# The order of the attention units in a hybrid encoder block: two heads by turns, scores by pairs

## The chip, the cores and the metric

The kernel runs on one core of a Trainium2 chip. Its time is the device time of one execution in microseconds (us), from the first to the last instruction and what lies around them; the metric is the median of several runs. The engines are the matrix engine (PE, with its weight loads shown apart as PEld), the vector engine (DVE), the scalar engine (ACT), GpSimd (POOL) and the engine that issues the transfers (SP). Each has an instruction stream of its own, and they meet through semaphores.

## What is computed

One layer of an encoder with 1024 tokens of width 1024. One projection gives the columns of two groups of eight heads of 64, and each group's output is gated and projected back:

```python
h = x @ w_in                                   # q_a k_a v_a z_a q_b k_b v_b z_b
y_a = neighborhood_attention(q_a, k_a, v_a, rel_bias)      # 2-D window 8 x 16 on a 16 x 64 grid
y_b = windowed_gqa_with_sink(rotary(q_b), rotary(k_b), v_b, sink)   # |i - j| <= 128, 2 kv heads
mixed = concat(y_a * silu(z_a), y_b * silu(z_b))
x = layer_norm(alpha * x + mixed @ w_out)
```

In the b group a softmax row also holds a learned sink logit. In the a group a learned bias is added to each score.

## The kernel before, in words

All products are made in 16-bit pieces: a value is split into a high and a low half, and a product is the sum of high times high, high times low and low times high. A projection of 128 columns thus takes 2 x 24 matmuls of 512 columns (L405).

Three stages follow each other: values and the first six projections (to about 123 us), the attention (to about 357 us), and the output projection with the layer norm (`final`). The remaining 15 projections and the first products of the output are not a stage of their own: they are a list of work, `FILL`, from which `pump_to` takes a share at each step of the attention, by the step numbers in `FILL_AT`, so that PE always has something to do.

The attention consists of 128 units, written out in `unit_list`, and its loop has a step for each. A unit is 128 queries of one head. Heads go by pairs p = 0 to 3, with j = 0 or 1 in the pair. The b group comes first: 16 units for a pair, first the eight query blocks i of j = 0, then those of j = 1. A block looks at three key blocks (384 columns), blocks 0 and 7 at two (256). The a group has 16 units for a pair too: for each j four column strips b (windows of 24, 32, 32 and 24 grid columns) of two row halves each.

At step i the loop does this, in program order, which every engine keeps (the stage is written in a manual schedule):

- `stage_load` for unit i + 7: for an a unit of half 0 and b not 2 it issues the bias load (L878) and queues the scaling on POOL (L882). A ring of BR = 5 buffers holds the biases.
- `stage_qk(i)`: two matmuls into one of four PSUM banks "s" that are used in turn, q against the high keys (L910) and q against the low keys (L911). q holds its high half in 64 rows and its low half in the other 64, and the keys lie in both, so that one product over 128 rows gives two of the terms. Then one DVE instruction adds mask or bias and finds the row's extreme (L920); for b units of blocks 0 and 1 a copy of one column puts the sink in place first (L915).
- for the quad whose turn it is (four units in a row, nine steps after its first unit): `stage_ot` of the quad before (four transposes on PE, L995, and the product with the gate, L998 or L1004), `stage_pv` (the weighted sums, 33 or 36 matmuls of 64 columns, L975).
- `stage_tr(i - 1)`: the high half of the probabilities on ACT (L946), the low half on DVE (L947), and a transposing transfer (L950). L947 is the last reader of the score bank.
- `stage_on` one step after `stage_pv`: reciprocal and product with the row sums (L981, L984).
- `stage_exp(i)`: the exponential on ACT (L936), written back into the score bank.

Around these the loop takes operations from queues for ACT, DVE, POOL and SP: the evacuation of finished projections (L281 to L289 and L319 for q and k, L335 to L339 for the rotary, L362 to L366 for gates), the splitting of the next weights, transfers. `need` puts out at once what has not been taken when it is needed; before a unit it is called for the stacks of its head. The values of the a group are gathered from DRAM for the next pair (`gather_v`, L834) at the steps of `VA_STEP`.

Of the kernel before, what the change touches and what calls it, by code (L numbers as in the profile page):

```python
# [17 lines left out]
HD = 64  # L18
# [24 lines left out]
Z3_END = 119  # L43
WIN_AT = [186, 202, 218, 234]
VA_AT = [46, 49, 52, 55]
VA_STEP = [(0, 1, 1), (0, 1, 3), (1, 0, 1), (1, 0, 3)]
# [21 lines left out]
def hybrid_block(ctx, tc, xT, x, wt, wv, wo, bias, sink, gain, lbias, cos, sin, bmask, out):  # L68
# [238 lines left out]
    def split_k(p, half, src, dep=None):  # L307
        sl = slice(512 * half, 512 * half + 512)
        ops = []
        prio = 0 if dep is None else 1  # L310
        eng = "pool" if dep and clock["step"] is not None else "dve"
        for j in range(2):
            a, o = slice(64 * j, 64 * j + 64), slice(64 - 64 * j, 128 - 64 * j)
            hi, lo = split_hl(lambda j=j, a=a: own("kh", p, j)[a, sl], lambda j=j, a=a: own("kl", p, j)[a, sl],
                              src[a], dep is None, eng)

            def dup_(w, j=j, a=a, o=o):
                t = own(w, p, j)
# [5 lines left out]
            dup = [enq("pool", lambda d=dup_: d("kh"), o1, after=32 if dep else 0),  # L324
                   enq("pool", lambda d=dup_: d("kl"), o2, after=36 if dep else 0)]
            stk_ops.setdefault((p, j, half), []).extend(dup)
        return ops

# [529 lines left out]
    on = {}  # L858

    def geom(u):  # L860
        g, p, j, t, _ = u
        if g == "a":
            b, half = t
            w = WINW[b]
            return NKEY[b], [4 * w] * 3
        lo, hi = max(t - 1, 0), min(t + 2, 8)
        return 128 * (hi - lo), [128] * (hi - lo)

    def stage_load(u, i):
        g, p, j, t, _ = u  # L870
        n, _c = geom(u)
        if g == "a":
            b, half = t
            if half == 0 and b != 2:
                bulk["last"] = clock["step"] + 1
                bt = ap.tile([128, 23 * WINW[1]], F32, tag="bs", name="bias", bufs=BR)
                o, m = BOFF[b], 23 * WINW[b]
                nc.sync.dma_start(bt[:, :m], bias[2 * p + j, :, o:o + m])  # L878
                bv = bt[:, :m]
                ld = Op("sp", None, [], 1)  # L880
                ld.step = i
                op = enq("pool", lambda: nc.gpsimd.tensor_scalar(bv, bv, rsg, -1.0, op0=ALU.mult, op1=ALU.mult),  # L882
                         ld, prio=0)
                st["bias"] = bt, op
            o = 11 * WINW[b] * half
            st[u, "b"] = st["bias"][0][:, o:o + NROW[half] * WINW[b]], st["bias"][1]

    def stage_qk(u):
        g, p, j, t, _ = u
        n, _c = geom(u)  # L890
        ps = bank("s")
        m, end = n, 384
        if g == "a":
            b, half = t
            m, end = NROW[half] * WINW[b], 384 if half else 384 - WINW[1]
            q = stks["q", p, j][:, 512 * half + 128 * b:512 * half + 128 * b + 128]
            sl = [stks[w, p, j].rearrange("p (r c) -> p r c", c=GW)[
                :, 4 * half:4 * half + NROW[half], WIN0[b]:WIN0[b] + WINW[b]] for w in ("kh", "kl")]
            bias_t, op = st.pop((u, "b"))
            need(op)  # L900
            init = 3e38
        else:
            q = stks["q", f"b{p}", j][:, 128 * t:128 * t + 128]
            lo = max(t - 1, 0) * 128
            kv = p // 2
            sl = [stks[w, "b", kv][:, lo:lo + n] for w in ("kh", "kl")]
# [3 lines left out]
        nc.tensor.matmul(ps[:, :m], q, sl[0], start=True, stop=False)  # L910
        nc.tensor.matmul(ps[:, :m], q, sl[1], start=False, stop=True)  # L911
        s0 = sns[units.index(u) % 2]
        sn = s0[:, end - m:]
        if g == "b" and t < 2:
            nc.vector.tensor_copy(s0[:, 384:385], nsk[:, h:h + 1])  # L915
# [4 lines left out]
        nc.vector.tensor_tensor_reduce(sn[:, :m], ps[:, :m], bias_t, sg[:, c:c + 1], init,  # L920
                                       op0=ALU.add, op1=ALU.min, accum_out=nm)
        st[u, "sn"] = sn
        st[u, "ps"] = ps
        st[u, "nm"] = nm

    def stage_exp(u):
        n, _c = geom(u)
        m = n + 1 if u[0] == "b" else n
        sn, nm = st.pop((u, "sn")), st.pop((u, "nm"))
        pt = st.pop((u, "ps"))  # L930
        k = units.index(u) % 4
        if k == 0:
            st["sm"] = ap.tile([128, 4], F32, tag="sm", name="sm", bufs=4)
        sm = st["sm"]
        st[units.index(u) // 4, "sm"] = sm
        nc.scalar.activation(pt[:, :m], sn[:, :m], AF.Exp, bias=nm, scale=-1.0, accum_out=sm[:, k:k + 1])  # L936
        st[u, "p"] = pt

    def stage_tr(u):
        g, p, j, t, _ = u  # L940
        n, ch = geom(u)
        pt = st.pop((u, "p"))
        c, m = ch[0], len(ch)
# [7 lines left out]
        st[u, "tr"] = tr  # L951

    def quad(q):
        g, p, j, t, _ = units[4 * q]
        return g, p, j, t // 4 if g == "b" else t[0] // 2

    def stage_pv(q):
        ps = st[q, "o"] = bank("t")
        for m in range(4):
            u = units[4 * q + m]  # L960
            g, p, j, t, _ = u
            n, ch = geom(u)
            tr = st.pop((u, "tr"))
            c = ch[0]
# [1 line left out]
            for i in range(len(ch)):  # L966
# [4 lines left out]
                    v = [vb[:, max(t - 1, 0) + i, p // 2, e, :] for e in range(2)]  # L971
                ph, pl = tr[:c, 2 * i, :], tr[:c, 2 * i + 1, :]
                mms += [(ph, v[0]), (ph, v[1]), (pl, v[0])]
            for i, (a, b_) in enumerate(mms):
                nc.tensor.matmul(ps[:, HD * m:HD * m + HD], a, b_, start=(i == 0), stop=(i == len(mms) - 1))  # L975

    def stage_on(q):
        g, p, j, h = quad(q)
        ps = st.pop((q, "o"))
        ri = ap.tile([128, 4], F32, tag="ri", name="ri", bufs=4)  # L980
        nc.vector.reciprocal(ri, st.pop((q, "sm")))  # L981
        if j == 0:
            on[g, p, h] = ap.tile([128, 4, 2, HD], F32, tag="on", name="on", bufs=2)
        nc.vector.tensor_mul(on[g, p, h][:, :, j, :], ps[:, :4 * HD].rearrange("p (m e) -> p m e", e=HD),  # L984
                             ri.unsqueeze(2).to_broadcast([128, 4, HD]))

    def stage_ot(q):
        g, p, j, h = quad(q)
        if j == 0:
            return  # L990
        need(*stk_ops.get(f"zb{p}" if g == "b" else f"z{p}", ()))
        ps = bank("t")
        o = on.pop((g, p, h))
        for i in range(4):
            nc.tensor.transpose(ps[:, 128 * i:128 * i + 128], o[:, i].rearrange("p h e -> p (h e)"), identf)  # L995
# [275 lines left out]
    for i in range(-LD, NU + LO):  # L1271
# [31 lines left out]
        if bulk["last"] != i or (queues["sp"] and i - queues["sp"][0].born > 2):  # L1303
            pop("sp", 1 if i < 118 else 3)
        if i < NU:
            u = units[i]
            if u[3] in (0, 4):
                need(*stk_ops[f"b{u[1]}", u[2], u[3] // 4])
            if u[3] == (0, 0):
                need(*stk_ops[u[1], u[2], 0], *stk_ops[u[1], u[2], 1])  # L1310
            stage_qk(u)
        q, m = divmod(i - LP - 3, 4)
        if i >= Q30 + 2:
            q, m = (NU // 4 - 2, i - Q30 - 2) if i < Q30 + 4 else divmod(i - LP - 3, 4)
        elif i >= Q30:
            q, m = -1, 0
        if m == 0 and 0 <= q - 1 < NU // 4:
            stage_ot(q - 1)
        if m == 0 and 0 <= q < NU // 4:
            stage_pv(q)  # L1320
        if i > Z3_END:
# [9 lines left out]
            wo_scale(i - WO_MAX - 4)  # L1331
        pump_to(i + F1)
        if 0 <= q < NU // 4:
            g, p, j, h = quad(q)
# [90 lines left out]
```

## Time and profile before

| what | us |
|---|---|
| median of 3 runs | 447.07 |
| lowest and highest | 446.6, 447.26 |
| the profiled execution | 447.43 |
| its span, first to last instruction | 445.6 |
| PE busy | 438.6 |
| PEld busy | 254.3 |
| DVE busy | 345.7 |
| ACT busy | 309.0 |
| POOL busy | 227.0 |

Busy times of different engines lie beside each other. A matmul's row shows when it started; its length is modelled and longer than the distance to the next start, because matmuls are pipelined. In a view of groups stand line, engine, operation, output and inputs, shape, count, busy time, mean ns of one, and the idle time ahead of them with what ended it. In a view in order of time stand start, length and the instruction, and in brackets the idle time before it. In a view of stretches stand the stretch, its length, the busy time of PE, PEld, DVE, ACT and POOL with their counts, the granted clock of PE, the share of the DMA engines and GB/s. A row of transfers ends with KB each, where it is known, and the median us from issue to landing.

### The profile page before, as it was taken

The page shows a single profiled execution, that of the slowest core. Times are in us where ns is not written, and L with a number is a line of the kernel's source. Part 1 is how long each engine was busy: PE and PEld are TensorE (multiplying, and loading weights), DVE is VectorE, ACT ScalarE, POOL GpSimd, SP SyncE. Part 2 cuts the span into 40 slices and gives each one's busy share as a digit, 9 for nine tenths or more (in the row PEclk, how much of TensorE's full clock was granted, in tenths as well). Part 3 has the DMA queues.
Part 4 walks back from the last instruction along what each step waited for, and adds up shares of the span by engine and source line. Part 5 has one row for each costly group of instructions (what it writes and reads, how often), then busy time and mean ns, then how long its engine had stood idle before and what let it go on. Part 6 is the DMA issues. An engine that isn't in the chain of part 4 may idle for free.

```text
span 445.6 us, 9522 instructions
## 1 busy us (share of the span) xinstructions
PE 438.6 (98%) x3271; PEld 254.3 (57%) x3271; DVE 345.7 (78%) x862; ACT 309.0 (69%) x718; POOL 227.0 (51%) x240
## 2 busy tenths in 40 slices
PE   9999999999999999999999999999999999999994
PEld 8996754444445555565655655655555654444442
DVE  5969967829989787786898888897767747279954
ACT  6769459877488998798979978797886876002211
POOL 0002753565837758868507628667762446005740
PEclk9999999999999999999999999999999999999999
DMA  8972068976847887678989999999999888101721
GB/s 306 348 286 94 1 242 270 298 268 238 285 138 165 149 179 163 141 146 133 165 164 173 194 182 184 201 188 239 189 189 229 156 190 323 49 0 71 253 79 71
DMA packets 133984, 81.76 MB, mean 183 GB/s; under 512 B 101296, under 2 KB 113328, under 8 KB 133680
## 3 DMA queue, kind: packets, MB, share of 16 engines
q1 hardware_dynamic: 133504, 80.67, 74.1%
q8 instruction: 25, 0.41, 0.4%
q10 hardware_dynamic: 432, 0.49, 0.3%
q14 instruction: 23, 0.19, 0.2%
HBM read 50.73 MB, written 9.96 MB: 136 GB/s over the span
## 4 chain that ended last, share of the span: by engine, by line
PE 88%; DMA 6%; ACT 3%; DVE 1%; issue 0%; SPq 0%; ACTq 0%; DVEq 0%
PE ps_pj L405 47%; PE ps_s L1122 9%; PE ps_t L975 7%; PE ps_pj L1122 5%; PE ps_t L1122 5%; PE ps_s L910 4%; PE ps_s L911 4%; PE ps_s L662 3%; PE ps_t L995 2%; PE ps_t L662 1%; DMA wos<-in_wo 1%; PE ps_pj L662 1%; DMA wr<-in_wt 1%; DMA x<-in_xT 1%; ACT wf L511 1%; DMA wvraw<-in_wv 1%
## 5 line engine op out<-in xcount | busy, mean ns | idle before, releaser
L405 PE MATMUL ps_pj<-xf,wh 128*128 128x512 f16 x672 | 202.6, 379 | 0.1
L405 PE MATMUL ps_pj<-xf,wl 128*128 128x512 f16 x336 | 127.3, 379 | 0.0
L405 PEld LDWEIGHTS <-wh 128*128 128x128 f16 x672 | 63.9, 98 | 60.3 <-issue 0.5
L936 ACT ACTIVATE ps_s<-sn,nm 128x385 f32<-128x385 f32 (+3 forms) x128 | 70.0, 547 | 28.9 <-DVE nm L920 27.8
L947 DVE SCALAR_TENSOR_TENSOR split<-ps_s,split 128x384 f16<-128x384 f32 (+2 forms) x128 | 65.6, 512 | 16.9 <-ACT split L946 16.0
L1122 PEld LDWEIGHTS <-m 128*128 128x128 f16 x408 | 38.8, 98 | 42.7 <-issue 0.2
L946 ACT ACTIVATE split<-ps_s 128x384 f16<-128x384 f32 (+2 forms) x128 | 57.6, 450 | 2.4
L405 PEld LDWEIGHTS <-wl 128*128 128x128 f16 x336 | 32.9, 98 | 36.7
L920 DVE CUSTOM_DVE_ANT_0 sn<-ps_s,bias,sg 128x264 f32<-128x264 f32 (+1 forms) x64 | 35.2, 549 | 15.8 <-PE ps_s L911 5.3
L212 POOL TENSOR_SCALAR wr<-wr,wsc 128x512 f32<-128x512 f32 x26 | 22.1, 851 | 41.1 <-ACT wh L207 35.5
L920 DVE CUSTOM_DVE_ANT_0 sn<-ps_s,bm,nsk 128x384 f32<-128x384 f32 (+1 forms) x64 | 40.7, 636 | 1.8 <-PE ps_s L911 1.3
L1122 PE MATMUL ps_s<-wo,m 128*128 128x512 f16 (+1 forms) x192 | 42.0, 372 | 0.0
L910 PE MATMUL ps_s<-ks,qs 128*128 128x384 f16 (+4 forms) x128 | 39.2, 306 | 0.0
L882 POOL TENSOR_SCALAR bias<-bias,rsg 128x552 f32<-128x552 f32 (+1 forms) x24 | 18.7, 779 | 40.3 <-DMA bias<-in_bias 32.0
L911 PE MATMUL ps_s<-ks,qs 128*128 128x384 f16 (+4 forms) x128 | 39.2, 306 | 0.0
L975 PEld LDWEIGHTS <-tr 128*128 128x128 f16 (+1 forms) x1104 | 36.6, 98 | 2.2
L1179 ACT ACTIVATE sd<-mv,eps 128x1 f32<-128x1 f32 x8 | 2.4, 295 | 44.3 <-DVE mv L1177 42.0
L213 POOL TENSOR_TENSOR wl<-wr,wh 128x512 f16<-128x512 f32 x26 | 31.6, 1215 | 2.2
L1221 POOL TENSOR_TENSOR xr<-xr,gb 128x512 f32<-128x512 f32 x7 | 11.2, 1608 | 39.7 <-ACT xr L1218 39.7
L319 POOL COPY ks<-ks 64x512 f16<-64x512 f16 x40 | 26.0, 662 | 4.7 <-DVE ks L289 1.8
L558 POOL TENSOR_SCALAR xraw<-xraw,xsc 128x512 f32<-128x512 f32 x3 | 4.9, 1645 | 41.0 <-ACT xf L553 41.0
L1122 PE MATMUL ps_pj<-wo,m 128*128 128x512 f16 (+1 forms) x120 | 25.2, 347 | 0.0
(208 smaller groups left out, 840.3 us busy)
## 6 DMA issues: line engine op xcount, KB each, us to landing
ws<-in_wt SPq DMA_DIRECT2D x15, 512.0 KB, 5.7
wr<-in_wt SPq DMA_DIRECT2D x26, 256.0 KB, 3.7
bias<-in_bias SPq DMA_DIRECT2D x16, 276.0 KB, 3.4
wor<-in_wo SPq DMA_DIRECT2D x16, 256.0 KB, 3.6
xr<-in_x SPq DMA_DIRECT2D x8, 512.0 KB, 8.1
xraw<-in_xT SPq DMA_DIRECT2D x15, 256.0 KB, 5.0
out<-xr SPq DMA_DIRECT2D x14, 256.0 KB, 2.1
bias<-in_bias SPq DMA_DIRECT2D x8, 368.0 KB, 3.8
```

What stands on the lines that cost most here:

```text
L213: nc.gpsimd.tensor_sub(l, raw, h)
L319: nc.gpsimd.tensor_copy(t[o, sl], t[a, sl])
L405: nc.tensor.matmul(ps, a[:, k % 4, :], mv, start=(k == 0 and i == 0), stop=(k == KT - 1 and i == 2))
L662: nc.tensor.matmul(ps[:, :320], lh[1, k][:, 128 * t:128 * t + 128], rh[k][:, 320 * a:320 * a + 320], start=(k == 0 and i == 0), stop=(k == ...
L910: nc.tensor.matmul(ps[:, :m], q, sl[0], start=True, stop=False)
L911: nc.tensor.matmul(ps[:, :m], q, sl[1], start=False, stop=True)
L920: nc.vector.tensor_tensor_reduce(sn[:, :m], ps[:, :m], bias_t, sg[:, c:c + 1], init, op0=ALU.add, op1=ALU.min, accum_out=nm)
L936: nc.scalar.activation(pt[:, :m], sn[:, :m], AF.Exp, bias=nm, scale=-1.0, accum_out=sm[:, k:k + 1])
L946: nc.scalar.activation(hl[:, :m, 0, :c], src, AF.Copy, scale=PSCALE)
L947: nc.vector.scalar_tensor_tensor(hl[:, :m, 1, :c], src, PSCALE, hl[:, :m, 0, :c], op0=ALU.mult, op1=ALU.subtract)
L975: nc.tensor.matmul(ps[:, HD * m:HD * m + HD], a, b_, start=(i == 0), stop=(i == len(mms) - 1))
L1122: nc.tensor.matmul(ps, lh[:, ts], rh[:, cs], start=(e == EO[0] and i == 0), stop=(e == EO[-1] and i == 2))
```

## The change

The units of a pair alternate between its heads: in the b group block i of j = 0, then block i of j = 1; in the a group, for each strip, (half, j) = (0, 0), (1, 1), (0, 1), (1, 0). The score products of two units are put out together at every even step, high keys for both and then low keys for both; the rest of `stage_qk` stays at the unit's own step. The stacks of both heads are asked for ahead of the pair's first unit. The sink's column is copied for block 0 alone, since each head now keeps its own of the two score tiles. A quad now holds both heads, so its output goes into one half of a tile of eight, and `stage_ot` follows for two quads at once, at every odd quad. Biases are kept for each j, loaded when the strip changes, in a ring of six. Values are gathered one strip a quad.

```diff
-LTT, LPP, BP, BH, BR, ND, NA, NX, F1 = 1, 6, 2, 9, 5, 1, 1, 6, 0.2
+LTT, LPP, BP, BH, BR, ND, NA, NX, F1 = 1, 6, 2, 9, 6, 1, 1, 6, 0.2
...
         for p in range(4):
-            for j in range(2):
-                for i in range(8):
-                    us.append(("b", p, j, i, i % 2 == 1))
+            for i in range(8):
+                for j in range(2):
+                    us.append(("b", p, j, i))
         for p in range(4):
-            for j in range(2):
-                for b in range(4):
-                    for half in range(2):
-                        us.append(("a", p, j, (b, half), half == 1))
+            for b in range(4):
+                for half, j in ((0, 0), (1, 1), (0, 1), (1, 0)):
+                    us.append(("a", p, j, (b, half)))
...
-            if half == 0 and b != 2:
+            key = p, j, b - (b == 2)
+            if st.get(("bias", j), (None,))[0] != key:
...
+    def stage_mm(us):
+        for u in us:
+            m, q, sl = qk_parts(u)
+            ps = st[u, "ps"] = bank("s")
+            nc.tensor.matmul(ps[:, :m], q, sl[0], start=True, stop=False)
+        for u in us:
+            m, q, sl = qk_parts(u)
+            nc.tensor.matmul(st[u, "ps"][:, :m], q, sl[1], start=False, stop=True)
...
-        nc.tensor.matmul(ps[:, :m], q, sl[0], start=True, stop=False)
-        nc.tensor.matmul(ps[:, :m], q, sl[1], start=False, stop=True)
...
-        if g == "b" and t < 2:
+        if g == "b" and t == 0:
             nc.vector.tensor_copy(s0[:, 384:385], nsk[:, h:h + 1])
...
-        if j == 0:
-            on[g, p, h] = ap.tile([128, 4, 2, HD], F32, tag="on", name="on", bufs=2)
-        nc.vector.tensor_mul(on[g, p, h][:, :, j, :], ps[:, :4 * HD].rearrange("p (m e) -> p m e", e=HD),
+        if q % 2 == 0:
+            on[q // 2] = ap.tile([128, 2, 4, HD], F32, tag="on", name="on", bufs=2)
+        nc.vector.tensor_mul(on[q // 2][:, q % 2], ps[:, :4 * HD].rearrange("p (m e) -> p m e", e=HD),
...
         if i < NU:
-            u = units[i]
-            if u[3] in (0, 4):
-                need(*stk_ops[f"b{u[1]}", u[2], u[3] // 4])
-            if u[3] == (0, 0):
-                need(*stk_ops[u[1], u[2], 0], *stk_ops[u[1], u[2], 1])
-            stage_qk(u)
+            if i % 2 == 0:
+                us = units[i:i + 2]
+                for u in us:
+                    if u[3] in (0, 4):
+                        need(*stk_ops[f"b{u[1]}", u[2], u[3] // 4])
+                    if u[0] == "a" and i % 16 == 0:
+                        need(*stk_ops[u[1], u[2], 0], *stk_ops[u[1], u[2], 1])
+                stage_mm(us)
+            stage_qk(units[i])
...
-        if m == 0 and 0 <= q - 1 < NU // 4:
-            stage_ot(q - 1)
+        if m == 0 and (3 <= q < NU // 4 and q % 2 == 1 or q == NU // 4):
+            stage_ot(q - 3 if q < NU // 4 else q - 2)
...
-            if g == "a" and p < 3 and (j, h, m) in VA_STEP:
-                gather_v(p + 1, VA_STEP.index((j, h, m)))
+            if g == "a" and p < 3 and m == 1:
+                gather_v(p + 1, b)
```

More of the change, by code (lines that the diff above doesn't have):

```diff
@@ L860, in geom @@
     def geom(u):
-        g, p, j, t, _ = u
+        g, p, j, t = u
         if g == "a":
@@ L883, in stage_load, with qk_parts @@
                          ld, prio=0)
-                st["bias"] = bt, op
+                st["bias", j] = key, bt, op
             o = 11 * WINW[b] * half
-            st[u, "b"] = st["bias"][0][:, o:o + NROW[half] * WINW[b]], st["bias"][1]
+            _, bt, op = st["bias", j]
+            st[u, "b"] = bt[:, o:o + NROW[half] * WINW[b]], op
+    def qk_parts(u):
+        g, p, j, t = u
+        n, _c = geom(u)
+        if g == "a":
+            b, half = t
+            q = stks["q", p, j][:, 512 * half + 128 * b:512 * half + 128 * b + 128]
+            sl = [stks[w, p, j].rearrange("p (r c) -> p r c", c=GW)[
+                :, 4 * half:4 * half + NROW[half], WIN0[b]:WIN0[b] + WINW[b]] for w in ("kh", "kl")]
+            return NROW[half] * WINW[b], q, sl
+        q = stks["q", f"b{p}", j][:, 128 * t:128 * t + 128]
+        lo = max(t - 1, 0) * 128
+        return n, q, [stks[w, "b", p // 2][:, lo:lo + n] for w in ("kh", "kl")]
+    def stage_mm(us):
[6 more added lines that the diff above has]
+            nc.tensor.matmul(st[u, "ps"][:, :m], q, sl[1], start=False, stop=True)
     def stage_qk(u):
-        g, p, j, t, _ = u
+        g, p, j, t = u
         n, _c = geom(u)
-        ps = bank("s")
+        ps = st[u, "ps"]
         m, end = n, 384
@@ L973, in stage_pv @@
                 mms += [(ph, v[0]), (ph, v[1]), (pl, v[0])]
+            o = HD * slot(u)
             for i, (a, b_) in enumerate(mms):
-                nc.tensor.matmul(ps[:, HD * m:HD * m + HD], a, b_, start=(i == 0), stop=(i == len(mms) - 1))
+                nc.tensor.matmul(ps[:, o:o + HD], a, b_, start=(i == 0), stop=(i == len(mms) - 1))
     def stage_on(q):
-        g, p, j, h = quad(q)
         ps = st.pop((q, "o"))
```

40 lines of the change are left out of this document (16 added, 24 removed).

## The prediction

> **What bounds the kernel now.** I read the page first, then busy time by stretch, then the matrix engine's instructions in order of time.
>
> ```profile
> span 445.6 us, 9522 instructions
> PE 438.6 (98%) x3271; PEld 254.3 (57%) x3271; DVE 345.7 (78%) x862; ACT 309.0 (69%) x718; POOL 227.0 (51%) x240
> ...
> PE 88%; DMA 6%; ACT 3%; DVE 1%; issue 0%; SPq 0%; ACTq 0%; DVEq 0%
> ```
>
> The chain that ended last is 88% PE. A stretch of the attention (busy time of PE, PEld, DVE, ACT, POOL) leaves PE no idle time, and vector and scalar engine little:
>
> ```profile
> 123.00:153.00 30.00, 29.89 (x238) 16.19 (x236) 25.60 (x83) 26.29 (x65) 19.32 (x18) 1.00 0.69 150
> 183.00:213.00 30.00, 30.00 (x268) 17.09 (x264) 22.27 (x64) 25.54 (x70) 21.98 (x23) 1.00 0.79 141
> ```
>
> Ends of matmuls are modelled, so 98% alone proves nothing; the starts do. PE in order of time, around units 47 to 49 (start, length, line, shape):
>
> ```profile
> 208.86 0.27 PE L910 MATMUL ps_s<-ks,qs 128*128 128x256 f16 x1
> 208.97 0.27 PE L911 MATMUL ps_s<-ks,qs 128*128 128x256 f16 x1
> 209.08 0.59 PE L405 MATMUL ps_pj<-xf,wh 128*128 128x512 f16 x2
> 209.51 0.38 PE L405 MATMUL ps_pj<-xf,wl 128*128 128x512 f16 x1
> ...
> 210.37 0.27 PE L910 MATMUL ps_s<-ks,qs 128*128 128x256 f16 x1
> 210.48 0.27 PE L911 MATMUL ps_s<-ks,qs 128*128 128x256 f16 x1
> ...
> 211.89 0.33 PE L910 MATMUL ps_s<-ks,qs 128*128 128x384 f16 x1
> 212.05 0.33 PE L911 MATMUL ps_s<-ks,qs 128*128 128x384 f16 x1
> ```
>
> Two products of 512 columns start 0.43 us apart (209.08 to 209.51), 0.215 us each; 256 columns take 0.11 (210.37 to 210.48), 384 take 0.16 (211.89 to 212.05). That is 0.42 to 0.43 ns a column throughout: PE streams without holes. Weight loads are hidden, and the second product into a bank is no dearer than the first. So PE work sets the time, and a wait of PE in the attention lengthens it one for one.
>
> The Trainium skill, Perfetto Trace Analysis, section Identifying the Most-Contended Engine, calls matmul busy time a bad measure of headroom and takes the busy share of weight loads instead, here 57%. By it PE would have much to gain from regrouping; the trace, with its even spacing, disagrees.
>
> **The change, part by part.**
>
> *Products.* Each unit keeps its two score products with the same columns, its weighted sums and its share of the transposes. Removed and added PE work is 0 us. Only the order is new: at an even step kh(i), kh(i+1), kl(i), kl(i+1), at an odd step none. PE starts even steps when it did before.
>
> *Score banks.* This is the disputed cost. There are four "s" banks, unit u uses bank u mod 4, and the bank is free when L947 (the low half of the split) of unit u-4 has read it. Before, an odd unit u asks for its bank at its own step. Now it asks one step earlier, right behind kh(u-1). Even units ask as before. So for each odd u I compare the end of L947 of unit u-4 with the score product of u-1. Unit 49 first (DVE in order of time):
>
> ```profile
> 209.55 0.69 DVE L366 SCALAR_TENSOR_TENSOR z<-z,ps_pj 128x512 f32<-128x512 f32 x1 [1.73 <-ACT z L365]
> 210.15 0.67 DVE L920 CUSTOM_DVE_ANT_0 sn<-ps_s,bm,nsk 128x384 f32<-128x384 f32 x1
> 210.75 0.55 DVE L947 SCALAR_TENSOR_TENSOR split<-ps_s,split 128x384 f16<-128x384 f32 x1
> 211.76 0.53 DVE L920 CUSTOM_DVE_ANT_0 sn<-ps_s,bm,nsk 128x256 f32<-128x256 f32 x1
> ```
>
> The 256-column L920 is unit 47 (block 7). The L947 ahead of it belongs to unit 45 and ends at 210.75 + 0.55 = 211.30. Unit 49 asked at 211.89: 0.59 us to spare. Now it asks at 210.37 + 0.11 = 210.48: **0.82 us too early**. Unit 45 is that late for a reason the change leaves in place (ACT, then POOL):
>
> ```profile
> 208.83 0.69 ACT L365 ACTIVATE z<-ps_pj,invt 128x512 f32<-128x512 f32 x1 [1.60 <-POOL rp_raw L337]
> 207.53 1.27 POOL L337 TENSOR_TENSOR rp_raw<-rp_raw,cos 128x512 f32<-128x512 f32 x1
> ```
>
> The gate of zb3 goes into the tile of the cosines, so it waits for the last rotary product at 208.80, and the exponential of unit 45 is queued behind it. The other two places are units 9 and 17:
>
> ```profile
> 136.56 0.27 PE L910 MATMUL ps_s<-ks,qs 128*128 128x256 f16 x1
> 137.86 0.33 PE L910 MATMUL ps_s<-ks,qs 128*128 128x384 f16 x1
> 136.65 0.55 DVE L947 SCALAR_TENSOR_TENSOR split<-ps_s,split 128x384 f16<-128x384 f32 x1
> 149.94 0.27 PE L910 MATMUL ps_s<-ks,qs 128*128 128x256 f16 x1
> 149.90 0.55 DVE L947 SCALAR_TENSOR_TENSOR split<-ps_s,split 128x384 f16<-128x384 f32 x1
> ```
>
> Unit 5 frees its bank at 136.65 + 0.55 = 137.20; unit 9, due at 137.86, would ask at 136.56 + 0.16 = 136.72 (unit 8 has 384 columns in the new order): 0.48 short. Unit 13 frees at 150.45; unit 17 would ask at 149.94 + 0.11 = 150.05: 0.40 short. Over these units DVE lags PE, so both count from one baseline: not 0.88 but the larger.
>
> The order also shifts where blocks 0 and 7 (256 columns, L920 0.53 instead of 0.67 us, about 0.27 with L947) fall: units 0, 1, 14, 15 of a pair instead of 0, 7, 8, 15. Unit 1 is lighter, so 0.27 less at unit 9; by unit 13 one light unit fewer has run, 0.27 more at unit 17 (0.67). For the first two places I take the middle, 0.5. For unit 49 the lighter unit 33 may bring the chain 0.27 forward: 0.82 - 0.27 = 0.55. Whether the two add depends on DVE having caught up with PE between them; I add them, since a shift of PE then moves the evacuations behind it too.
>
> In the second group the room is larger. Unit 64 asks at 239.51, and unit 61 (the L947 here, before block 7's) ends at 238.90:
>
> ```profile
> 239.51 0.28 PE L910 MATMUL ps_s<-ks,qs 128*128 128x264 f16 x1
> 238.34 0.56 DVE L947 SCALAR_TENSOR_TENSOR split<-ps_s,split 128x384 f16<-128x384 f32 x1
> ```
>
> Unit 65 then has 0.61 + 0.11 us in hand, so from here on I count 0.
>
> *The start.* PE waits once behind unit 0, for a projection bank:
>
> ```profile
> 123.59 0.27 PE L911 MATMUL ps_s<-ks,qs 128*128 128x256 f16 x1
> 123.98 0.59 PE L405 MATMUL ps_pj<-xf,wh 128*128 128x512 f16 x2
> 123.24 0.69 DVE L366 SCALAR_TENSOR_TENSOR z<-z,ps_pj 128x512 f32<-128x512 f32 x1 [0.29 <-ACT z L365]
> ```
>
> Instead of 0.11 it takes 0.39 to the next start, 0.28 of waiting. Two more products of 0.11 now lie in this hole: -0.22. The baseline above is absolute and already holds it, so it counts only if units 9 and 17 do not wait.
>
> *Earlier needs.* Both heads' stacks are needed at the pair's first unit, eight steps sooner for the second head. The tightest are the first pair's q (DVE) and q2 (DVE, then PE at unit 96):
>
> ```profile
> 120.32 2.63 DVE L289 TENSOR_TENSOR qs<-rp_raw,qs 64x512 f16<-64x512 f32 x2
> 295.34 0.69 DVE L287 SCALAR_TENSOR_TENSOR qs<-ps_pj,qs 64x512 f16<-64x512 f32 x1
> 298.29 0.28 PE L910 MATMUL ps_s<-ks,qs 128*128 128x264 f16 x1
> ```
>
> They end at 122.95, ahead of unit 0 at 123.48 (0.11 before the row of 123.59), and at 296.03, ahead of 298.29: 0 us, with 0.5 and 2.3 us of cover.
>
> *Vector engine.* Eight one-column copies go, one a pair for each head:
>
> ```profile
> L915 DVE COPY sn<-nsk 128x1 f32<-128x1 f32 x16 | 2.3, 144 | 0.0
> ```
>
> That is 8 x 0.144 = 1.2 us of DVE over the whole attention, beside PE: 0. The gate products move up to four steps later, to every second quad.
>
> *Transfers.* The 24 bias loads and 16 value gathers keep their number and sizes. Bias loads now come at two steps running instead of spread (lead 7 steps as before, a sixth buffer):
>
> ```profile
> bias<-in_bias SPq DMA_DIRECT2D x16, 276.0 KB, 3.4
> va<-vwin SPq DMA_DIRECT2D x8, 256.0 KB, 3.4
> tr<-split SPq DMA_TRANSPOSE x128, 3.3
> ...
> L882 POOL TENSOR_SCALAR bias<-bias,rsg 128x552 f32<-128x552 f32 (+1 forms) x24 | 18.7, 779 | 40.3 <-DMA bias<-in_bias 32.0 <-DVE split L947 6.8 <-ACT ks L281 0.7
> ```
>
> Seven steps of 1.81 us (unit 0 to 64 took 116.0) are 12.7 us against 3.4 and the 0.78 of scaling, so hidden. The transpose of a quad's last unit is issued five steps, 9 us, ahead of its product, and odd units now come no later. Both bias loads fall on steps before that transpose's, not beside it. SP's queue carries the same issues. If its cover were lost, a quad would wait about one bias landing, 3.4 us; I take 0.
>
> *Sum.* +0.5 (units 9, 17) + 0.55 (unit 49) = **+1.05 us**. The profiled execution took 447.43 us (span 445.6 and 1.8 around it), so 448.5 for itself; it lay 0.36 above the median of 447.07, so **448.1** in terms of the median. Bounds of the bank cost: -0.22 if no odd unit waits (the start's gain), 0.67 + 0.82 = 1.5 if DVE gains nothing, more in the second rival.
>
> **The rivals.**
>
> *The head start pays for itself (not slower).* Place: L920 of odd units. With the scores a step early DVE never waits for PE at an odd step, and if it runs ahead at every such step the L947 of units 5, 13 and 45 end earlier. It decides from a gain of 0.5 us at the first two places. Then only unit 49's 0.55 is left, less the start's 0.22: +0.33, 447.4; with that gone too, 446.85. For it: late steps of the attention, where DVE has caught up. Against it: at units 9 and 17 DVE is late by its own work, and 25.6 of 30 us busy leaves it little to gain.
>
> *Bubbles that repeat (slower still).* A late pair holds up two L920 at once, DVE empties and then has two units to do before the next pair, so the debt comes back in each of the four head pairs of the first group: 4 x 0.82 = 3.3 us, 450.4. For it: ACT has 26.29 of 30 us busy. Against it: a delayed PE gives DVE and ACT that very time to catch up. The Trainium skill, Perfetto Trace Analysis, section Optimization Strategy, says that a gap repeating on the engine that should be saturated can mean too little PSUM for the next tile; the trace of before shows no such gap, with one unit more in hand.
>
> *PE gets cheaper* by alternating banks or stationary operands: the spacing above leaves nothing to win beyond the start's 0.22 and small waits, 446.8 or a little under.
>
> **How the numbers follow.** Forecast 0.42, own range 447.6 to 449.2; head start 0.30; repeating bubbles 0.20; something slower that I do not see (a late transpose, 3.4 us a time) 0.03; faster 0.05. A measurement of this kernel can tell about 0.2%, 0.9 us, from no change. Slower by more (over 447.96): most of the forecast 0.36, 0.20 and 0.03, 0.59. Within: 0.30 and 0.06, 0.36. Faster: 0.05. The range reaches from the head start's lower end to the repeating bubbles, 446.8 to 450.6.
>
> **What would show it.** Right: PE gaps of 0.2 to 0.9 us between kh of an even unit and kh of the next one, near units 9, 17 and 49, ended by DVE L947, and spacing inside the pair unchanged (0.11, 0.16). PE's work the same, x3271. The wait at 123.59 smaller. Wrong: no gap there (head start); gaps in every pair (bubbles); PE waiting at the weighted sums for a transpose, or at the first unit of a pair for its stacks; or fewer PE instructions.

## The result and the profile after

The changed kernel takes 450.44 us, median of 8 runs (450.06 to 451.9), beside 447.14 (8 runs) for the kernel before: ratio 1.0074, 95% interval 1.0055 to 1.0093, **slower by 0.74% or 3.3 us**. The forecast was 448.1, slower by 1.05 us, range 446.8 to 450.6. Sign and place were right, the price was a third of the real one. The profiled execution took 450.34.

The page of the changed kernel: head line, busy times, and the chain that ended last.

```profile
span 448.6 us, 9494 instructions
PE 438.7 (98%) x3271; PEld 253.7 (57%) x3271; DVE 346.2 (77%) x854; ACT 309.0 (69%) x718; POOL 227.5 (51%) x240
...
PE 62%; DVE 13%; issue 8%; POOL 6%; ACT 6%; DMA 3%; SPq 0%; POOLq 0%; DVEq 0%; ACTq 0%
...
L908 PE MATMUL ps_s<-ks,qs 128*128 128x384 f16 (+4 forms) x128 | 29.6, 306 | 2.6 <-DVE split L962 2.5
L911 PE MATMUL ps_s<-ks,qs 128*128 128x384 f16 (+4 forms) x128 | 28.7, 306 | 0.0
```

PE has as many matmuls and as much busy time as before (438.6), but it no longer makes up 88% of the chain: DVE, POOL and ACT now hold 25% of it, because PE waits for them. In the two last rows (lines have moved: L908 was L910, the high-key product; L962 was L947, the low split; L936 was L920, L951 was L936; of the lines up to L800 each was one higher, so L404 was L405 and the gate's L364 and L365 were L365 and L366) the products with the high keys wait, and for the low split, as forecast; those with the low keys never do. Busy time by stretch shows where:

```profile
123.00:153.00 30.00, 28.50 (x200) 14.84 (x199) 25.88 (x81) 24.82 (x61) 18.55 (x18) 1.00 0.75 148
183.00:213.00 30.00, 29.28 (x263) 16.64 (x261) 21.82 (x61) 25.55 (x69) 22.66 (x25) 1.00 0.77 139
239.00:357.00 118.00, 118.00 (x1089) 69.08 (x1087) 95.37 (x274) 96.90 (x248) 73.87 (x92) 1.00 1.00 193
```

The loss lies in the first group, early and near unit 49; over the whole second group PE has no idle time. PE in order of time at the five odd units that wait (7, 9, 13, 17, 49):

```profile
132.82 0.33 PE L908 MATMUL ps_s<-ks,qs 128*128 128x384 f16 x1
133.38 0.32 PE L908 MATMUL ps_s<-ks,qs 128*128 128x384 f16 x1 [0.24 <-DVE split L962]
...
136.46 0.79 PE L908 MATMUL ps_s<-ks,qs 128*128 128x384 f16 x2
137.09 0.32 PE L911 MATMUL ps_s<-ks,qs 128*128 128x384 f16 x1
...
143.47 0.33 PE L908 MATMUL ps_s<-ks,qs 128*128 128x384 f16 x1
144.66 0.32 PE L908 MATMUL ps_s<-ks,qs 128*128 128x384 f16 x1 [0.87 <-DVE split L962]
...
151.17 0.27 PE L908 MATMUL ps_s<-ks,qs 128*128 128x256 f16 x1
151.69 0.27 PE L908 MATMUL ps_s<-ks,qs 128*128 128x256 f16 x1 [0.25 <-DVE split L962]
...
212.01 0.27 PE L908 MATMUL ps_s<-ks,qs 128*128 128x256 f16 x1
213.43 0.27 PE L908 MATMUL ps_s<-ks,qs 128*128 128x256 f16 x1 [1.15 <-DVE split L962]
```

The bracket understates a gap, since the length of the matmul ahead of it is modelled. Take the distance of the starts less the spacing of the columns: 133.38 - 132.82 - 0.16 = 0.40 at unit 7; 1.03 at unit 13; 0.41 at unit 17; 1.31 at unit 49. At unit 9 the two are folded into one row; the next start less two spacings gives 137.09 - 136.46 - 0.32 = 0.31. Sum 3.46. At the start, the wait of 0.28 is gone:

```profile
123.19 0.38 PE L908 MATMUL ps_s<-ks,qs 128*128 128x256 f16 x2
123.41 0.38 PE L911 MATMUL ps_s<-ks,qs 128*128 128x256 f16 x2
123.63 0.59 PE L404 MATMUL ps_pj<-xf,wh 128*128 128x512 f16 x2
```

The projection follows after two spacings of 0.11. 3.46 - 0.28 = 3.2, against 3.3 between the medians: as near as the medians tell, the loss is in these five gaps.

**Where the two large ones come from.** DVE, then POOL, ahead of unit 13 in the changed kernel, then the same two in the kernel before:

```profile
141.71 1.22 DVE L785 TENSOR_TENSOR zcol<-vscb,msc 128x1 f32<-128x1 f32 x2
...
144.07 0.54 DVE L962 SCALAR_TENSOR_TENSOR split<-ps_s,split 128x384 f16<-128x384 f32 x1
```
```profile
141.69 1.15 POOL L212 TENSOR_TENSOR wl<-wr,wh 128x512 f16<-128x512 f32 x1
```
```profile
141.43 0.23 DVE L786 TENSOR_TENSOR zcol<-vscb,msc 128x1 f32<-128x1 f32 x2
...
142.79 0.56 DVE L947 SCALAR_TENSOR_TENSOR split<-ps_s,split 128x384 f16<-128x384 f32 x1
```
```profile
141.66 1.16 POOL L213 TENSOR_TENSOR wl<-wr,wh 128x512 f16<-128x512 f32 x1
```

L785 is two products of one column each, the last of a chain of scale computations (`m_scale`) that the loop spreads over steps 2 to 9. Before, they ran in 0.23 us, and POOL's product of 512 columns started as they ended (141.43 + 0.23 = 141.66). Now they start 0.02 us behind it and end at 142.93, when POOL's is over (142.84): 1.22 us. The low split of unit 9 behind them ends at 144.61 instead of 143.35, and unit 13 starts 0.05 us later. The Trainium skill, SBUF — State Buffer, section Who interferes with whom, has a rule for this: a DVE instruction with two inputs in SBUF and a GpSimd instruction that reads SBUF exclude each other, and whichever starts first keeps the port for its whole length. The trace agrees where POOL starts first. The pair of before does not show the other order: POOL starts 0.09 us behind its own instruction ahead (140.88 + 0.69 = 141.57), and the next one follows it as closely (142.82, 142.90), so no wait for DVE is to be seen there. e3 below shows both orders.

Ahead of unit 49 the order of ACT, then of DVE, in the changed kernel:

```profile
210.98 0.69 ACT L364 ACTIVATE z<-ps_pj,invt 128x512 f32<-128x512 f32 x1 [1.59 <-POOL rp_raw L336]
211.57 0.58 ACT L951 ACTIVATE ps_s<-sn,nm 128x385 f32<-128x385 f32 x1
```
```profile
211.70 0.69 DVE L365 SCALAR_TENSOR_TENSOR z<-z,ps_pj 128x512 f32<-128x512 f32 x1 [1.12 <-ACT z L364]
212.30 0.54 DVE L936 CUSTOM_DVE_ANT_0 sn<-ps_s,bm,nsk 128x256 f32<-128x256 f32 x1
...
212.82 0.56 DVE L962 SCALAR_TENSOR_TENSOR split<-ps_s,split 128x384 f16<-128x384 f32 x1
```

It is the wait that the prediction named: the gate of zb3 waits 1.59 us for the tile of the cosines, the exponential of unit 45 stands behind it, and its low split ends at 213.38 (before: 211.30, so 2.08 later, while unit 48, at 212.01 instead of 210.37, came only 1.64 later).

### The profile page after: what moved, and what is told of

It is laid out like the page before. It is cut to its first block, busy times and chain, and to the rows that moved or that the text cites. A ratio compares the mean times of both kernels' runs of the same rounds, so it can differ in the third digit from the quotient of the medians.

```text
span 448.6 us, 9494 instructions
## 1 busy us (share of the span) xinstructions
PE 438.7 (98%) x3271; PEld 253.7 (57%) x3271; DVE 346.2 (77%) x854; ACT 309.0 (69%) x718; POOL 227.5 (51%) x240
## 4 chain that ended last, share of the span: by engine, by line
PE 62%; DVE 13%; issue 8%; POOL 6%; ACT 6%; DMA 3%; SPq 0%; POOLq 0%; DVEq 0%; ACTq 0%
PE ps_pj L404 25%; PE ps_s L1136 9%; PE ps_t L991 6%; PE ps_pj L1136 5%; PE ps_t L1136 5%; POOL wl L212 3%; PE ps_s L908 3%; PE ps_s L911 3%; PE ps_s L607 2%; ACT ps_s L951 2%; POOL wr L211 2%; DVE sn L936 2%; ACT split L961 1%; DVE wf L513 1%; PE ps_t L1009 1%
## 5 line engine op out<-in xcount | busy, mean ns | idle before, releaser
L404 PE MATMUL ps_pj<-xf,wh 128*128 128x512 f16 x672 | 201.8, 379 | 0.0
L404 PE MATMUL ps_pj<-xf,wl 128*128 128x512 f16 x336 | 127.3, 379 | 0.0
L404 PEld LDWEIGHTS <-wh 128*128 128x128 f16 x672 | 63.9, 98 | 64.4 <-issue 0.2
L951 ACT ACTIVATE ps_s<-sn,nm 128x385 f32<-128x385 f32 (+3 forms) x128 | 70.0, 547 | 32.5 <-DVE nm L936 31.3
L962 DVE SCALAR_TENSOR_TENSOR split<-ps_s,split 128x384 f16<-128x384 f32 (+2 forms) x128 | 65.5, 512 | 20.9 <-ACT split L961 20.5
L404 PEld LDWEIGHTS <-wl 128*128 128x128 f16 x336 | 32.9, 98 | 37.5
L936 DVE CUSTOM_DVE_ANT_0 sn<-ps_s,bias,sg 128x264 f32<-128x264 f32 (+1 forms) x64 | 35.1, 548 | 14.5 <-PE ps_s L911 13.8
L211 POOL TENSOR_SCALAR wr<-wr,wsc 128x512 f32<-128x512 f32 x26 | 22.0, 848 | 42.6 <-ACT wh L206 37.0
L936 DVE CUSTOM_DVE_ANT_0 sn<-ps_s,bm,nsk 128x384 f32<-128x384 f32 (+1 forms) x64 | 40.6, 635 | 3.3 <-PE ps_s L911 3.2
L908 PE MATMUL ps_s<-ks,qs 128*128 128x384 f16 (+4 forms) x128 | 29.6, 306 | 2.6 <-DVE split L962 2.5
L911 PE MATMUL ps_s<-ks,qs 128*128 128x384 f16 (+4 forms) x128 | 28.7, 306 | 0.0
```

What stands on the lines that cost most here:

```text
L211: nc.gpsimd.tensor_scalar(raw, raw, scale, 1.0, op0=ALU.mult, op1=ALU.mult)
L404: nc.tensor.matmul(ps, a[:, k % 4, :], mv, start=(k == 0 and i == 0), stop=(k == KT - 1 and i == 2))
L911: nc.tensor.matmul(st[u, "ps"][:, :m], q, sl[1], start=False, stop=True)
L962: nc.vector.scalar_tensor_tensor(hl[:, :m, 1, :c], src, PSCALE, hl[:, :m, 0, :c], op0=ALU.mult, op1=ALU.subtract)
```

## The experiments

The theory after the result: putting products out in pairs costs PE nothing in itself; what costs is that each odd unit asks a step early at the few places where its bank is late, and two late readers (L785 behind POOL, the gate of zb3) make up two thirds of the price. The rivals: the new order of units costs in itself; the bubbles repeat; PE loses in the pairs as such. All gaps of the profiled executions in one table, in us (gaps over 0.07 that the kernel before does not have, the start included; the account is their sum less the 0.28 at the start before; measured is the difference of medians to the runs of the kernel before on the same chip):

| kernel | start | 7 | 9 | 13 | 17 | 49 | others | account | measured | ratio, 95% interval |
|---|---|---|---|---|---|---|---|---|---|---|
| changed | 0 | .40 | .31 | 1.03 | .41 | 1.31 | | 3.2 | 3.3 | 1.0074 (1.0055-1.0093) |
| e1 | 1.74 | | | .27 | .19 | | | 1.9 | 0.4 | 1.001 (0.9996-1.0023) |
| e2 | .68 | .08 | .47 | | | .91 | .50 | 2.4 | 1.7 | 1.0042 (1.0026-1.0057) |
| e3 | | | | .32 | .88 | | 10.7 | 11.6 | 12.0 | 1.0278 (1.0245-1.0311) |
| e4 | | | .16 | .78 | 1.36 | .41 | 1.78 | 4.2 | 3.9 | 1.0084 (1.0059-1.0109) |
| e5 | | .40 | .31 | 1.00 | .40 | 1.29 | | 3.1 | 3.3 | 1.0077 (1.0062-1.0093) |
| e6 | | .40 | | | 2.09 | 1.29 | .09 | 3.6 | 3.5 | 1.0079 (1.0067-1.0091) |
| e7 | .33 | .40 | | | 2.10 | 1.29 | | 3.8 | 4.0 | 1.009 (1.0077-1.0103) |
| e8 | .33 | .40 | .36 | | .12 | 1.02 | .37 | 2.3 | 2.1 | 1.0045 (1.0032-1.0058) |
| e10 | | .40 | .42 | | .40 | 1.29 | | 2.2 | 2.5 | 1.0054 (1.0038-1.0071) |
| e11 | | .40 | .31 | .99 | .41 | | | 1.8 | 2.1 | 1.0049 (1.0032-1.0065) |
| e12 | .59 | | | .29 | .19 | | | 0.8 | 0.8 | 1.0018 (1.0004-1.0031) |
| e13 | | .41 | .47 | | .15 | | .38 | 1.1 | 1.7 | 1.0037 (1.0023-1.0052) |

But for e1, whose profiled execution (449.31) was far above its median (447.58), the account gives the measured difference within 0.7 us. The rest lies ahead of the attention: unit 0 starts between 122.65 and 123.50 in these executions, at 123.48 in that of before. With that shift added, the account gives the difference between each profiled execution and that of the kernel before (447.43) within 0.1 us, e1 included; for the changed kernel 3.18 - 0.29 = 2.89, measured 450.34 - 447.43 = 2.91. So the gaps account for the time. The intervals of the ratios are mostly some 0.3% wide (1.3 us) and many overlap, so what a single edit takes away is read from the gaps.

**e1: the new order, scores at each unit's own step.**

```diff
-            if i % 2 == 0:
-                us = units[i:i + 2]
...
-                stage_mm(us)
+            u = units[i]
...
+            stage_mm([u])
```

> The changed kernel with one thing undone: each unit's two score products are put out at its own step again; order of the units, loads, gates as changed. If the score bank that is asked for a step early is the cause, the PE gaps ended by the low split vanish and the time falls back to that of before, 446.9 to 447.6. If the new order itself costs (heavy blocks in a run, earlier stacks, loads by two), it stays near 450, at least above 449.

447.58, +0.1% and not told from no change, as expected. The new order alone costs at most 0.23%; small gaps stay at units 13 and 17. In its profiled execution the projection behind unit 0 waits 1.57 us for a gate's evacuation:

```profile
123.46 0.27 PE L911 MATMUL ps_s<-ks,qs 128*128 128x256 f16 x1
125.30 0.59 PE L404 MATMUL ps_pj<-xf,wh 128*128 128x512 f16 x2 [1.57 <-DVE z L365]
```

This wait differs between kernels' executions from 0 to 1.74 us (column "start"); why was not found.

**e2: pairs in the old order.** The kernel before, with its units as they were, but with `stage_mm` for two at even steps.

> The kernel before with the other part alone: old order of the units, scores of two units multiplied together at every second step. If the early request is the cause by itself, PE gaps near units 9, 17 and 49 of 0.3 to 0.9 us each, in sum about 1.3, less 0.2 at the start: 448.0 to 448.5. If the loss needs the new order as well, no gap and 447.0. If early requests alone make it all, 450.

448.92, more than expected. The pairs without the new order cost 0.42%. PE at unit 49 in it:

```profile
211.27 0.27 PE L905 MATMUL ps_s<-ks,qs 128*128 128x256 f16 x1
212.28 0.32 PE L905 MATMUL ps_s<-ks,qs 128*128 128x384 f16 x1 [0.74 <-DVE split L959]
```

1.01 - 0.11 = 0.90 (0.91 by unrounded starts): near the 0.82 that the prediction read from the trace of before without any term for the order. Unit 13 does not wait. Nor does unit 17, which the trace of before has 0.40 short: PE had lost 0.36 at unit 5 (in "others"), 0.08 at 7 and 0.47 at 9 by then, as the prediction's one baseline says. e1 and e2 add to 0.52%, the change costs 0.74%; the intervals do not tell these apart, but the gaps do: 1.03 at unit 13 is in neither of the two (0.27 in e1, none in e2) and came only with the order and the pairs together.

**e3: probabilities in SBUF.** The exponential writes a tile in SBUF, so the score bank is free after L936; the bias ring goes back to 5 for the room.

```diff
-        pt = st.pop((u, "ps"))
+        st.pop((u, "ps"))
+        pt = ap.tile([128, 388], F32, tag="pt", name="pt", bufs=3)
```

> The changed kernel, but the exponential writes its result to a tile in SBUF instead of back into the score bank, so that the bank is free when the mask and extreme have been taken, some 2 to 4 us sooner (one bias buffer fewer to make room). If the bank is the cause, no PE gap at odd units is left and the time is 446.8 to 447.5, unless split instructions on SBUF are slower or meet POOL. If the order is the cause, near 450.

459.22, a miss: the remedy was dearer than the illness. Groups of e3, then of the kernel before:

```profile
L963 DVE SCALAR_TENSOR_TENSOR split<-pt,split 128x384 f16<-128x384 f32 x80 | 64.4, 805 | 10.6 <-ACT split L962 10.5
```
```profile
L947 DVE SCALAR_TENSOR_TENSOR split<-ps_s,split 128x384 f16<-128x384 f32 x80 | 44.3, 554 | 11.3 <-ACT split L946 10.9
```

The low split takes 805 ns instead of 554 when both its operands lie in SBUF. This is the meeting with POOL again. Of the 80 splits in e3, the 21 that start while POOL runs nothing take 554 ns in the mean, the 59 that start beside a POOL instruction 894; 47 of these last 0.61 to 1.48 us, and each of them ends 0.40 to 0.42 us after that instruction does. In the changed kernel, with one operand in PSUM, those that start beside POOL take 554 as well. One split of each kind in e3, each with the POOL instruction that it meets:

```profile
182.48 1.48 DVE L963 SCALAR_TENSOR_TENSOR split<-pt,split 128x384 f16<-128x384 f32 x1
197.85 0.56 DVE L963 SCALAR_TENSOR_TENSOR split<-pt,split 128x384 f16<-128x384 f32 x1
```
```profile
182.28 1.27 POOL L336 TENSOR_TENSOR rp_raw<-rp_raw,cos 128x512 f32<-128x512 f32 x1
197.87 1.10 POOL L211 TENSOR_SCALAR wr<-wr,wsc 128x512 f32<-128x512 f32 x1
```

In the first POOL leads and the split lasts; in the second the split leads by 0.02 us and L211 takes 1.10 us, where the fastest of its kind in e3 takes 0.69. DVE falls behind everywhere. The gaps at units 7, 9 and 49 are gone, but the others make 11.9 us, 4.6 of them behind the transposes of the outputs and 2.8 at score products that wait for L936 (units 13 and 17 among them). So the time says nothing on the theory.

**e4: half a dose.** The second unit's products half a step later.

```diff
-                stage_mm(us)
+                stage_mm(us[:1])
...
         pump_to(i + F1)
+        if i < NU and i % 2 == 0:
+            pump_to(i + 0.5)
+            stage_mm(units[i + 1:i + 2])
```

> The changed kernel, but the second unit of a pair is multiplied half a step later, behind half of the even step's projection products (some 0.8 us later than in the pair). If the bank request decides, each gap of the changed kernel (0.40, 0.31, 1.03, 0.41, 1.31 us) shrinks by up to 0.8: about 0.7 us of gaps left, 447.6. If regrouping as such costs, it stays near 450.

451.11, slower than the whole dose: inconclusive as a sum, because the edit also moved evacuations of projections in program order. At unit 17 the gate's L365 now stands ahead of an L936 that it stood behind, and waits for ACT (0.75 us) in DVE's queue; the gap there rose from 0.41 to 1.36. In "others" lie 1.33 at a weighted sum of the second group and 0.44 at unit 16. Unit 49, where no such thing moved, does answer, in PE's order of time:

```profile
212.50 0.27 PE L908 MATMUL ps_s<-ks,qs 128*128 128x256 f16 x1
...
213.15 0.38 PE L404 MATMUL ps_pj<-xf,wl 128*128 128x512 f16 x1
213.78 0.27 PE L908 MATMUL ps_s<-ks,qs 128*128 128x256 f16 x1 [0.25 <-DVE split L962]
```

Unit 49 asks 0.87 us behind unit 48 (213.15 + 0.22 - 212.50) instead of 0.11, and the gap is 0.41 instead of 1.31: 0.76 of the 0.90 is the later asking.

**e5: the gate of zb3 tied to the cosine product**, so that it should not be queued ahead of the exponential of unit 45.

```diff
-        o = enq("act", lambda: nc.scalar.activation(zt[e][:, sl], ps, AF.Tanh, scale=half_inv), prio=0)
+        o = enq("act", lambda: nc.scalar.activation(zt[e][:, sl], ps, AF.Tanh, scale=half_inv),
+                tiles["cos_op"] if name == "zb3" else None, prio=0)
```

> The changed kernel, with the gate of zb3 put out only after the last product with the cosines has been put out, so that ACT does not stand in front of the exponential of unit 45. Early bank request as the cause: the gap at unit 49 (1.31 us) shrinks to 0.3 or less, the four gaps near units 7 to 17 stay, 449.1 to 449.6. If the gap there has another cause, 450.4 and the gap unchanged.

450.29, a miss: the product had been put out already when the gate was taken, so nothing moved; ACT still waits 1.59 us and the gap is 1.29.

**e6: the scale computations eight steps later.**

```diff
-        if 2 <= i < 10:
-            m_scale(i - 2)
+        if 10 <= i < 18:
+            m_scale(i - 10)
```

> The changed kernel, with the eight small steps that make the scale of the gated outputs taken at steps 10 to 17 instead of 2 to 9. In the changed kernel two of their one-column products on DVE last 1.15 us together while POOL runs a product of its own, and unit 13's gap of 1.03 us follows. If that meeting of DVE and POOL sizes the gap, it shrinks to 0.3 or less and 449.4 to 449.8 results, unless the steps meet POOL elsewhere. If the gap is the pairing's own, 450.4 with the gap unchanged.

450.42, a miss: the gaps at 9 and 13 went, one of 2.09 at unit 17 came. DVE, then POOL, in e6:

```profile
148.59 1.48 DVE L773 TENSOR_TENSOR zg<-zg,wg 128x1 f32<-128x1 f32 x2
```
```profile
147.68 1.15 POOL L212 TENSOR_TENSOR wl<-wr,wh 128x512 f16<-128x512 f32 x1
148.79 1.26 POOL L338 TENSOR_TENSOR rp_raw<-rp_raw,rp_sw 128x512 f32<-128x512 f32 x1
```

Again one-column operations with two inputs in SBUF (here maxima) end as a POOL product ends (150.07 and 150.05). The meeting had moved, not gone.

**e7: e5 and e6 together.**

> Both of these edits in the changed kernel: gate of zb3 after the cosines, and the scale at steps 10 to 17. If the two are separate late readers of the score banks, the gains add: 448.2 to 448.9, with gaps of about 1 us in sum left near units 7 to 17. If they share a cause, no better than the better one of the two.

450.97, a miss: as e6, since e5 did nothing.

**e8: the light block earlier**, blocks in the order 0, 1, 2, 3, 7, 6, 5, 4, to change which units are light.

```diff
-            for i in range(8):
+            for i in (0, 1, 2, 3, 7, 6, 5, 4):
...
```

> The changed kernel with the blocks of the b group in the order 0, 1, 2, 3, 7, 6, 5, 4, so that light units (256 columns) stand at places 0, 1, 8 and 9 of sixteen, about as in the kernel before (0, 7, 8, 15). If twelve heavy units in a row make DVE and ACT later, the gaps at units 13, 17 and 49 shrink by 0.3 to 0.5 us each: 449.2 to 449.8. If the run of heavy units does not matter, 450.4.

449.01. L785 missed POOL's product and the gap at 13 is gone; at 49 it fell from 1.31 to 1.02, at 17 from 0.41 to 0.12: 0.29 at each, with two more light units ahead of each. Small ones of 0.1 came in the middle.

**e10: one-column products with a scalar operand.** The five two-tensor operations of `m_scale` become operations of a tensor with a scalar column.

```diff
-                    nc.vector.tensor_mul(zcol[:, 1 + i:2 + i], vscb[:, i:i + 1], msc)
+                    nc.vector.tensor_scalar_mul(zcol[:, 1 + i:2 + i], vscb[:, i:i + 1], msc)
```

> The changed kernel; the one-column products of the output scale on DVE are written with the factor as a scalar operand (tensor_scalar) instead of as a second tensor, the form that lasts 0.14 us beside a busy POOL in this profile. If the meeting of the two-tensor form with POOL sizes the gap at unit 13, none of these steps lasts over 0.3 us, the gap of 1.03 us falls under 0.3, and the time is 449.4 to 449.8. If the gap belongs to the pairing alone, 450.4.

449.22. DVE and POOL at the same place as above:

```profile
141.18 0.32 DVE L785 TENSOR_SCALAR zcol<-vscb,msc 128x1 f32<-128x1 f32 x2
```
```profile
141.17 1.16 POOL L212 TENSOR_TENSOR wl<-wr,wh 128x512 f16<-128x512 f32 x1
```

They start 0.01 us behind POOL's product and take 0.32 beside it. Only the form of the operands changed, and the gap at 13 went: 1.03 us shown. (The medians moved from +3.3 to +2.5 us; their intervals overlap.)

**e11: the gate of zb3 in a slot of its own** (bias ring of 5 for the room).

```diff
-ZTAG = {"z3": "zv", "zb3": "zc", "z2": "zs", "zb1": "zd", "zb2": "ze"}
+ZTAG = {"z3": "zv", "zb3": "zf", "z2": "zs", "zb1": "zd", "zb2": "ze"}
```

> The changed kernel, with the gate of zb3 in a place of its own instead of that of the cosines (five bias buffers instead of six to make room). If ACT's wait for the last product with the cosines makes the late release at unit 45, that wait (1.6 us) goes and the gap of 1.31 us at unit 49 falls under 0.3: 449.0 to 449.5. If something else holds unit 45, 450.4.

448.89. ACT, then PE at units 48 and 49:

```profile
208.96 0.68 ACT L364 ACTIVATE z<-ps_pj,invt 128x512 f32<-128x512 f32 x1
```
```profile
211.69 0.42 PE L908 MATMUL ps_s<-ks,qs 128*128 128x256 f16 x2
211.94 0.38 PE L911 MATMUL ps_s<-ks,qs 128*128 128x256 f16 x2
```

The gate has no wait. The first low-key product starts 0.25 us behind the first high-key one, 0.03 more than two spacings of 0.11: the gap at 49 is gone, 1.31 us shown. (The medians moved from +3.3 to +2.1 us; the intervals overlap here too.)

**e12: pairs in the second group only**, own steps in the first.

> The changed kernel with each unit's products at its own step in the first group (units 0 to 63) and in pairs in the second (64 to 127). If pairing only costs where the bank is late, the second group costs nothing: 447.2 to 447.9, like all units at their own step, and no PE gap after 240 us. If pairing has a price of its own, about half of the loss stays: 448.5 to 449.5.

447.56, which is 0.8 us above the kernel before on the same chip, beside 0.4 for e1; the intervals overlap. Its gaps lie at the start and at units 13 and 17, where nothing is paired. Busy time by stretch in the second group:

```profile
239.00:357.00 118.00, 118.00 (x1104) 69.41 (x1103) 96.19 (x276) 96.98 (x248) 72.05 (x90) 1.00 1.05 193
```

32 pairs without idle time of PE: a pair as such is free where no bank is late.

**e13: e8, e10 and e11 together**, pairs everywhere.

> The changed kernel, pairs kept, with three late readers taken away: scale products by scalar, the gate of zb3 in its own place, light units at places 0, 1, 8, 9. If the loss is the sum of early requests that meet late readers, only the gaps near units 7 and 9 (0.7 us) and small ones stay: 447.4 to 448.2. If pairing costs by itself, no less than 449.

448.47, a little above the expected range. Both large gaps are gone; 0.41 and 0.47 at units 7 and 9 stay, with small ones. Half the loss is recovered, not all, and the kernel before, at 446.75 beside it, is still the fastest of all.

## Why the prediction was right in kind and wrong in size

- *PE work, spacing, stacks, transfers at 0*: right. x3271, 438.7 us; 0.11 and 0.16 in pairs that do not wait; no gap of the changed kernel ends at a transpose, a bias or a stack.
- *Second group at 0*: right (118.00 of 118.00), and e12 shows it alone.
- *Start, -0.22*: the wait of 0.28 went, as said, and it was right that the absolute baseline holds it already: see the next point, which counts it.
- *Units 9 and 17, "not 0.88 but the larger", 0.5*: **the step that failed.** The one baseline held as far as unit 9: gaps at 7 and 9 less the start, 0.40 + 0.31 - 0.28 = 0.43, beside the 0.48 of the working. These two gaps need no further cause. The same reading of the trace of before has unit 7 short too, by 133.66 - 133.59 = 0.07, which the working did not name; PE gained the 0.28 of the start and DVE 0.04 ("head start" below), and 0.48 + 0.28 - 0.04 = 0.72, beside gaps of 0.71. In e10, where DVE is 0.07 later there instead, it is 0.83, beside 0.82.

  By unit 17 the term was too small. In e10, where L785 does not disturb, the early places make 0.40 + 0.42 + 0.40 - 0.28 = 0.94, where the working had 0.48 - 0.27 = 0.21 for unit 9 and 0.67 for unit 17 and took 0.5 as the middle (it is 0.44). It let the lighter unit 1 pay for one of the two units, 7 and 8, that became heavy; but DVE gained only 0.04 by unit 5. Without that, 0.40 + 2 x 0.27 = 0.94. This fits, and is not shown: e8, with two more light units ahead of unit 17, takes only 0.29 off the gap there (0.12 instead of 0.41), so a light unit brings less than 0.27.

  With L785 the early places make 2.15 - 0.28 = 1.87: another 0.93 for a meeting of DVE and POOL of which the trace of before shows only the near miss (DVE 0.23 us ahead of POOL). Neither the sum nor a bound had a term for it, and the trace of before left unit 13 only 143.41 - 143.35 = 0.06 to spare. The gap at 17 is the same behind it (0.41, in e10 0.40): while PE waits at unit 13 it falls back as far as DVE did, so DVE gains nothing.
- *Unit 49, 0.82 - 0.27 = 0.55*: right place, right cause (e11), wrong sign of the second term. Units 39 and 40 have 384 columns in the new order and had 256 before; by unit 45 only two light units of the pair had run instead of three, and the two that became heavy stand closer ahead of the late place than the one that became light (33). DVE was later against PE by 0.44 (2.08 - 1.64), not earlier by 0.27. The traces show the path, which runs over ACT and POOL: the exponential of unit 38 starts 1.60 us later than before (196.19, 194.59), about as PE does, ACT's step on a weight behind units 39 to 41 2.16 later (L206, first row below; before, second row), POOL goes on from that weight without a pause to the product with the cosines, and the gate waits for it (209.67 instead of 207.53, 2.14 later). What the light unit 33 brought, if anything, was gone by unit 38. With 0.82 the 0.44 gives 1.26; measured 1.31. e2, with the old order, has 0.91, and e8, with units 40 and 41 light, 1.02.

```profile
202.47 0.72 ACT L206 ACTIVATE wh<-wr,wsc 128x512 f16<-128x512 f32 x1
```
```profile
200.31 0.72 ACT L207 ACTIVATE wh<-wr,wsc 128x512 f16<-128x512 f32 x1
```
```profile
209.67 1.27 POOL L336 TENSOR_TENSOR rp_raw<-rp_raw,cos 128x512 f32<-128x512 f32 x1
```

- *The sum*: 0.5 and 0.55 became 0.94 + 0.93 and 1.31, together 3.18 for 1.05.
- *Bubbles that repeat, 450.4*: gave the very number and has the wrong mechanism. There are four gaps in the first two head pairs, none in the third, one in the fourth, and the two large ones have causes of their own. The measured 450.44 lies above the forecast's own range (447.6 to 449.2), and the wide range reaches it only through this rival: that is luck.
- *Head start*: no. The low split of unit 5 in the changed kernel, which releases unit 9:

```profile
136.32 0.55 DVE L962 SCALAR_TENSOR_TENSOR split<-ps_s,split 128x384 f16<-128x384 f32 x1
```

  It ends 13.68 us after the first score product (123.19); before, 137.20 - 123.48 = 13.72. DVE gained 0.04 there, not the 0.5 from which this rival decides. (In e10 it ends 13.79 us after.)
- *What stays open*: how much of the lateness at unit 17 is the heavy units', what half a step is worth at the early places (e4 moved other things), and the start's variation. A version with pairs and without any gap was not found.

## What to carry to other kernels

A ring of buffers has a slack for each user: from the end of the last reader to the moment of asking. To ask a step earlier spends that slack at every user, so it is read user by user, in the order that the change makes and not the old one. The price is set by the few readers that are late for other reasons, and each new lag counts again. Look also for near misses in the old trace: two instructions that only just did not meet can meet when one engine shifts by 0.3 us.

## What the hardware showed beyond that

- A DVE operation of one column with both operands in SBUF lasted until the end of the POOL product beside it (two took 1.22 us in the changed kernel behind one such product and 1.48 in e6 behind two; 0.23 in the kernel before, without the meeting); with a scalar operand it did not wait (0.32 for two beside POOL).
- The low split of 384 columns took 805 ns from SBUF and 554 ns from PSUM. The difference is the same meeting: from SBUF it took 554 ns too when POOL ran nothing at its start, and 894 when it started beside a POOL instruction.
